# GpSimd's final store waits in reversed order, in a layer norm without affine part

## Chip, cores, metric

The kernel runs on one core of a Trainium2 chip. The metric is the device time of one execution in microseconds, median of several. A profile's span goes from the core's first to its last recorded instruction; the time of a run of this kernel is some 1.8 to 1.9 us longer than its span. A wait is called **met** when its semaphore has reached the value waited for before the engine comes to it.

## The reference

```python
def setup_inputs():                 # x: 32 x 512 x 1024 float32, 67 MB
    ...
def reference(x, eps):
    mean = np.mean(x, axis=-1, keepdims=True)
    var = np.var(x, axis=-1, keepdims=True)
    return ((x - mean) / np.sqrt(var + eps)).astype(np.float32)
```

## The kernel before

The 16384 rows are cut into 17 tiles: fifteen of 8 rows per partition, one of 6, one of 2. A ring of 48 rows per partition holds six large tiles. SP issues the loads (ScalarE half of the first), VectorE takes the statistics, GpSimd combines them, ScalarE normalizes in place and issues the stores. Each store adds 16 to a semaphore `stored[t]`, and SP refills a place of the ring when its store has landed. Everything is inside one critical section. At its end GpSimd waits for those stores that nobody else waits for: tiles 10 to 16, the last owners of the ring.

```python
TILES = (8,) * 15 + (6, 2)
SLOT, SLOTS = 8, 6
...
    ctx.enter_context(tc.tile_critical(no_gpsimd_drain=True))
...
    # ScalarE, for every tile t
                nc.scalar.dma_start(
                    out=rows_of(o2, row, K)[:, a - at : a - at + n, :], in_=ring[:, a : a + n, :]
                )._wait_ge(act, row + k - at + 1).then_inc(stored[t], 16)
...
    for t in range(len(plan)):
        if t in owner.values():                       # tiles 10 to 16
            nc.gpsimd.wait_ge(stored[t], sixteens(stored, t))
# the critical section, then the kernel, ends here
```

## Time and profile before

| | before |
|---|---|
| time, median of 3 runs | 317.93 us (317.60 to 318.04) |
| span of the profiled run | 316.04 us |
| last increment of the last store's semaphore | 314.96 us |
| from there to the end of the span | 1.087 us |

The fourth row is what this document is about, and it is called the **tail**. It is read from the trace: the time of the sixteenth increment of `stored[16]`, taken from the end of the last recorded instruction. The profile's lines for this stretch are in the prediction.

### The profile page before, as it was taken

To read this page: it belongs to the slowest core of one execution; us is meant where nothing else is said; L and a number is where in the kernel's file an instruction comes from. 1 tells how busy PE (TensorE), PEld (TensorE's weight loads), DVE (VectorE), ACT (ScalarE), POOL (GpSimd) and SP (SyncE) were. 2 spreads that over 40 slices of the span, in tenths; PEclk is the share of its full clock that TensorE was granted. 3 is DMA by queue.
4 is the path that set the end of the run, shared out by engine and by line. 5 is a ranking of instruction groups with operands and counts; after the bars stand their busy time and mean duration, and the time that the engine had idled before them with its cause. 6 is when DMAs were issued, how large, how long until landed. Compare 5 with 4: busy or idle time off the path is not lost.

```text
span 316.0 us, 713 instructions
## 1 busy us (share of the span) xinstructions
DVE 156.4 (49%) x273; ACT 153.0 (48%) x146; POOL 41.7 (13%) x176
## 2 busy tenths in 40 slices
DVE  0296595956191651907529084380934709283000
ACT  1006695865834709256091651907429083383800
POOL 0002202022002020020200202011020110204300
DMA  7999999999999999999999999999999999999996
GB/s 294 435 460 402 452 406 402 461 398 465 399 466 402 460 415 448 431 431 452 411 456 406 456 406 456 406 460 402 464 402 460 406 441 452 429 434 425 448 399 285
DMA packets 5043, 134.24 MB, mean 425 GB/s; under 512 B 560, under 2 KB 560, under 8 KB 560
## 3 DMA queue, kind: packets, MB, share of 16 engines
q10 hardware_dynamic: 2592, 69.21, 50.9%
q1 hardware_dynamic: 2448, 65.01, 47.9%
q14 instruction: 3, 0.02, 0.0%
HBM read 67.11 MB, written 67.11 MB: 425 GB/s over the span
## 4 chain that ended last, share of the span: by engine, by line
DMA 61%; DVE 18%; ACT 9%; POOL 5%; issue 2%; ACTq 0%; DVEq 0%; POOLq 0%; SPq 0%
DMA ring<-in_x_dram 32%; DMA out_dram<-ring 29%; DVE stats L119 17%; ACT ring L215 9%; POOL rstd L187 1%; POOL dev L177 1%; POOL dev L181 1%; ACT std L205 0%; POOL dev L173 0%; POOL nmean L170 0%; POOL dev L174 0%; POOL half L166 0%; POOL half L182 0%; POOL nmean L167 0%; POOL ss L183 0%
## 5 line engine op out<-in xcount | busy, mean ns | idle before, releaser
L119 DVE BATCH_NORM_STATS2 stats<-ring 128x6 f32<-128x512 f32 x256 | 153.5, 677 | 86.1 <-DMA ring<-in_x_dram 85.5
L215 ACT ACTIVATE ring<-ring,nmr,rstd 128x1024 f32<-128x1024 f32 x128 | 146.6, 1226 | 11.2 <-POOL nmr L190 11.2
L205 ACT ACTIVATE std<-ss,eps_t 128x8 f32<-128x8 f32 (+2 forms) x17 | 5.1, 300 | 135.1 <-POOL ss L183 134.7
L166 POOL TENSOR_TENSOR half<-stats 128x16 f32<-128x16 f32 (+2 forms) x17 | 4.0, 233 | 232.3 <-DVE stats L119 232.3
L130 DVE RECIPROCAL rstd<-std 128x8 f32<-128x8 f32 x15 | 3.0, 203 | 48.5 <-ACT std L205 48.5
L177 POOL TENSOR_SCALAR dev<-dev 128x32 f32<-128x32 f32 (+2 forms) x17 | 5.0, 295 | 1.5
L190 POOL TENSOR_TENSOR nmr<-nmean,rstd 128x8 f32<-128x8 f32 (+2 forms) x17 | 3.5, 205 | 9.9 <-DVE rstd L130 9.7
L181 POOL TENSOR_TENSOR dev<-dev,stats 128x32 f32<-128x32 f32 (+2 forms) x17 | 4.3, 255 | 1.4
L173 POOL TENSOR_TENSOR dev<-stats,nmean 128x32 f32<-128x32 f32 (+2 forms) x17 | 4.1, 241 | 1.4
L174 POOL TENSOR_TENSOR dev<-dev 128x32 f32<-128x32 f32 (+2 forms) x17 | 4.0, 237 | 1.3
L170 POOL TENSOR_SCALAR nmean<-nmean 128x8 f32<-128x8 f32 (+2 forms) x17 | 4.0, 235 | 1.5
L182 POOL TENSOR_TENSOR half<-dev 128x16 f32<-128x16 f32 (+2 forms) x17 | 3.7, 215 | 1.3
L167 POOL TENSOR_TENSOR nmean<-half 128x8 f32<-128x8 f32 (+2 forms) x17 | 3.4, 202 | 1.3
L183 POOL TENSOR_TENSOR ss<-half 128x8 f32<-128x8 f32 (+2 forms) x17 | 3.4, 202 | 1.3
L187 POOL TENSOR_TENSOR rstd<-std,power 128x6 f32<-128x6 f32 (+1 forms) x2 | 2.1, 1042 | 3.0 <-ACT std L205 3.0
L205 ACT ACT_TABLE_LOAD x1 | 1.3, 1283 | 1.3 <-SPq L55 1.3
L134 DVE MEMSET eps_t<- 128x1 f32 x1 | 0.1, 59 | 1.0 <-SPq L55 1.0
L251 POOL MEMSET const-float32-0.0<- 128x1 f32 x1 | 0.1, 99 | 0.2 <-issue 0.2
L251 POOL MEMSET const-bfloat16-1.0<- 128x1 bf16 x1 | 0.1, 102 | 0.0
L251 POOL MEMSET const-uint8-127<- 128x1 uint8 x1 | 0.1, 102 | 0.0
L251 POOL MEMSET const-float32-1.0<- 128x1 f32 x1 | 0.1, 99 | 0.0
L135 DVE MEMSET power<- 128x8 f32 x1 | 0.1, 65 | 0.0
## 6 DMA issues: line engine op xcount, KB each, us to landing
out_dram<-ring ACTq DMA_DIRECT2D x15, 4096.0 KB, 46.4
ring<-in_x_dram SPq DMA_DIRECT2D x14, 4096.0 KB, 45.5
ring<-in_x_dram SPq DMA_DIRECT2D x1, 3072.0 KB, 43.1
out_dram<-ring ACTq DMA_DIRECT2D x1, 3072.0 KB, 16.0
ring<-in_x_dram ACTq DMA_DIRECT2D x1, 2048.0 KB, 12.6
ring<-in_x_dram SPq DMA_DIRECT2D x1, 2048.0 KB, 12.8
ring<-in_x_dram SPq DMA_DIRECT2D x1, 1024.0 KB, 54.8
out_dram<-ring ACTq DMA_DIRECT2D x1, 1024.0 KB, 14.3
```

The lines of the kernel that those rows point to most:

```text
L119: i = nc.vector.bn_stats(out=stats[:, at + k, s, :], in_=ring[:, at + k, s * BN_MAX : (s + 1) * BN_MAX],)
L166: then(0, g.tensor_tensor(out=h, in0=mean4[:, :, 0:2], in1=mean4[:, :, 2:4], op=ALU.add))
L170: g.tensor_scalar(out=nm, in0=nm, scalar1=-1.0 / H, scalar2=None, op0=ALU.mult),
L173: then(3, g.tensor_tensor(out=d, in0=mean4, in1=spread, op=ALU.add))
L174: then(4, g.tensor_mul(out=d, in0=d, in1=d))
L177: g.tensor_scalar(out=d, in0=d, scalar1=float(D // H), scalar2=None, op0=ALU.mult),
L181: then(6, g.tensor_tensor(out=d, in0=d, in1=m2, op=ALU.add))
L182: then(7, g.tensor_tensor(out=h, in0=d[:, :, 0:2], in1=d[:, :, 2:4], op=ALU.add))
L187: i = g.tensor_tensor(out=r, in0=std_t, in1=power[:, :K], op=ALU.pow)
L190: then(10, g.tensor_mul(out=nmr[:, at : at + K], in0=nm, in1=r), own)
L205: nc.scalar.activation(out=std[:, at : at + K], in_=ss[:, at : at + K], func=AF.Sqrt, bias=eps_t[:], scale=1.0 / D,)._wait_ge(*summed[t]). ...
L215: i = nc.scalar.activation(out=ring[:, k, :], in_=ring[:, k, :], func=AF.Identity, bias=nmr[:, k : k + 1], scale=rstd[:, k : k + 1],).then ...
```

## The change

The intent: after the last store has landed, as little as possible should still have to run. The compiler has made the seven waits into three instructions with two waits each (EVENT_SEMAPHORE in the profile, called wait instructions here) and puts the seventh wait on the branch that leaves the critical section. The first wait in the source's order gets the branch. In the old order that is tile 10, whose store landed 61 us earlier; in the new one it is tile 16, the last.

```diff
-    for t in range(len(plan)):
+    for t in reversed(range(len(plan))):
         if t in owner.values():
             nc.gpsimd.wait_ge(stored[t], sixteens(stored, t))
```

## The prediction

> **What bounds the kernel now.** I read the busy table first, then the DMA rows, then the DMA issues, the last microseconds of the timeline, and last the lines of the waiting instructions. The busy table and the DMA rows of the page say what sets nearly all of the time:
>
> ```profile
> DVE 156.4 (49%) x273; ACT 153.0 (48%) x146; POOL 41.7 (13%) x176
> ...
> DMA  7999999999999999999999999999999999999996
> ...
> HBM read 67.11 MB, written 67.11 MB: 425 GB/s over the span
> ```
>
> No engine is busy for half of the span, while the DMA engines are at 90% or more in every slice but the first and the last. The kernel moves 134 MB at 425 GB/s; that is 316 us. The change touches no transfer, so only the piece after the last byte can move. Where that piece begins is seen in the DMA issues and in the timeline of the last 16 us:
>
> ```profile
> out_dram<-ring ACTq DMA_DIRECT2D x1, 3072.0 KB, 16.0
> out_dram<-ring ACTq DMA_DIRECT2D x1, 1024.0 KB, 14.3
> ```
>
> ```profile
> 299.44 1.22 ACT L215 ACTIVATE ring<-ring,nmr,rstd 128x1024 f32<-128x1024 f32 x1
> 300.69 0.34 ACTq L227 DMA_DIRECT2D out_dram<-ring  x1
> ```
>
> The last store is issued at 300.69 and lands 14.3 us later, at 314.96; the one before it, issued at 296.49, landed at 312.53. The span ends at 316.04. So 1.09 us follow the last landing, and all that the change can touch lies in there. The views by source line show what stands there. First the line of the waits, then those of the end of the critical section and of the kernel's end (columns: line, queue, operation, count, shortest/median/longest duration in ns, first and last start in us):
>
> ```profile
> L234 POOLq EVENT_SEMAPHORE  x3: 42/43/43, 305.3 to 315.0; - x3
> ```
>
> ```profile
> L55 SPq EVENT_SEMAPHORE  x3: 17/17/9061, 235.3 to 292.2; - x3
> ...
> L55 POOLq COMPARE_BRANCH  x1: 38/38/38, 315.1 to 315.1; - x1
> L55 POOLq NOP  x1: 17/17/17, 315.2 to 315.2; - x1
> ```
>
> ```profile
> L265 POOLq EVENT_SEMAPHORE  x4: 17/17/17, 315.4 to 315.9; - x4
> ...
> L265 POOLq COMPARE_BRANCH  x1: 33/33/33, 0.7 to 0.7; - x1
> ```
>
> The reader is to see that GpSimd's seven waits (tiles 10 to 16, which last own a place of the ring) have become three wait instructions, not seven, and that a branch and a NOP of GpSimd follow them. The semaphores of these records, with times to the nanosecond, read:
>
> ```
> 312.553  0.043  event semaphore  waits stored[15], stored[12]
> 314.957         last of the 16 increments of stored[16]
> 314.980  0.043  event semaphore  waits stored[16], stored[11]
> 315.067  0.038  compare-branch   waits stored[10]
> 315.238  0.017  NOP, tells SP
> 315.281  0.013  SP's NOP, which waited for it
> 315.993  0.051  last record of the kernel's end (to 316.044)
> ```
>
> So three instructions carry two waits each, and the seventh wait rides on the branch that leaves the critical section. Written as a list in the source's order, 10 to 16, the branch takes the first and the three pairs are (14,13), (15,12), (16,11). The last store is thus waited for by the third wait instruction, and the branch runs after it although its own store landed at 253.78.
>
> [...] SP's pair on line 55 is recorded as 9061 ns long, most of it the wait for ScalarE. [...] Here GpSimd's branch is recorded as 38 ns and its successor starts 171 ns after it[...].
>
> **The change part by part.** It removes nothing and adds nothing: seven waits, on the same semaphores and values, in the opposite order. If the packing goes by place in the list, the branch takes the first of the new list, stored[16], and the pairs become (12,13), (11,14), (10,15). The number of instructions stays at three waits and a branch.
>
> What moves: the three pairs are done before the end. GpSimd's last arithmetic ends at 298.26; the pair (12,13) is done at once, (11,14) waits until 305.25, (10,15) until 312.53. Allowing 0.1 us for instructions, GpSimd stands at the branch by 312.65, 2.3 us before the last store lands. The branch then starts when a wait instruction would have, at 314.957 + 0.023 = 314.980, instead of 315.067. Removed from behind the last landing are one event semaphore, 0.043 us, and the gap from its end to the branch's start, 315.067 - 315.023 = 0.044 us: together 0.087 us.
>
> Does that reach the end? Everything after hangs on GpSimd: SP's NOP starts at 315.281, 26 ns after the end of GpSimd's NOP, SP's drain and then the closing barrier follow it, and no other engine arrives later on its own account (ScalarE and VectorE had entered the barrier by 301.3 and 292.2). So all of the 0.087 us should come off: 0.03% of 317.93. The sum is 317.93 - 0.09 = 317.84, called 317.85.
>
> **The rivals.** First, a branch that really waits could cost more than one that finds its wait met[...]. Then some of the 0.087 comes back[...]. Against it speaks the kernel's start, where GpSimd's branch on line 265 did wait, for SP: it started 25 ns after the end of SP's NOP, took 33 ns, and the next instruction began 153 ns after its start, not more than the 171 ns of the end. Read the other way, this would save up to 0.02 more: 317.82. The successors differ, so I count neither.
>
> Second, the compiler could order the waits by semaphore or pack them otherwise, so that the machine code is unchanged or the last store sits in a pair again. Then the time is 317.93. The pairs of before are mirrored by list place, which speaks for a rule by place, but since the list is also in order of semaphore number, this trace alone cannot exclude a sort. The title's statement that the branch now has the last store speaks against it.
>
> Third, a second wait within a pair might wake its engine late[...]. After the change stored[14] and stored[15] are such second waits. But there are 2.43 us between the landings of stored[15] and stored[16], so even a microsecond of it stays hidden: 317.84 still. Only stores landing in the other order would spoil this, and the last increments of the two stand 2.4 us apart.
>
> Fourth, the runs' own scatter hides the whole effect: three runs of before lie between 317.60 and 318.04, five times the expected gain. This I hold to be near certain for single runs.
>
> **Range and chances.** The mechanism gives 317.82 to 318.03 over all rivals. The median of a few runs adds some 0.2 us either way, and the median of before that I start from is itself of three runs only, so the range is 317.4 to 318.3. A change of 2% would be 6.4 us, six times all that lies behind the last landing, so faster by that much cannot come from here, and slower only if the transfers changed. Chances: 0.005 faster, 0.99 within 2%, 0.005 slower.
>
> **What would show it.** In the profile after, the line of the waits should still show three event semaphores, but two of them some 7 us long (from 298.4 to 305.3 and from 305.3 to 312.6, because their second waits are the late ones), with the last start at about 305.3 instead of 315.0. The branch on line 55 should start some 0.02 us after the last landing, and from the last landing to the span's end should take 1.00 us instead of 1.09. If that stretch is still 1.09 with the branch first, a waiting branch costs what was saved; if the last event semaphore still starts at the last landing, the packing is another. A time outside the range with that stretch as predicted would be a matter of the transfers and not of this change.

Passages that no trace of this case bears out are cut from the recorded texts (this one and those of `u_first` and `u_second`), and the cuts are marked. The forecast's sum loses no term by it: 317.93 - 0.043 - 0.044 = 317.84 us, called 317.85. Cut from the first rival is its worst case, 0.1 us beyond the 0.087, a guess that was not worked out from a trace. It made the upper end of the 317.82 to 318.03 us that the text gives for all rivals; without it that end is 317.93. The range of 317.4 to 318.3 stands.

## The result

| | before | after |
|---|---|---|
| time, median (6 runs each) | 317.75 us (317.60 to 318.04) | 317.69 us (317.58 to 318.38) |
| span of the profiled run | 316.044 us | 315.747 us |
| last increment of `stored[16]` | 314.957 us | 314.746 us |
| tail | 1.087 us | 1.001 us |

The ratio after to before is 1.000, with a 95% interval of 0.9987 to 1.0013. The forecast of 317.85 us, within 317.4 to 318.3, held; a kernel without any gain would have met it too.

The page of the kernel after shows the same DMA load:

```profile
DMA  7999999999999999999999999999999999999996
...
HBM read 67.11 MB, written 67.11 MB: 425 GB/s over the span
```

The lines of the wait instructions and of the end of the critical section, after (columns as in the prediction: line, queue, operation, count, shortest/median/longest duration in ns, first and last start in us):

```profile
L234 POOLq EVENT_SEMAPHORE  x3: 43/7250/7921, 297.0 to 305.1; - x3
```

```profile
L55 POOLq COMPARE_BRANCH  x1: 38/38/38, 314.8 to 314.8; - x1
L55 POOLq NOP  x1: 17/17/17, 314.9 to 314.9; - x1
```

Against 42/43/43 before, two of the three wait instructions now last 7.9 and 7.3 us, and the last of them starts at 305.1 instead of 315.0: the waiting is done in them, before the last landing. The semaphores and times in the trace, in us from the span's start, duration behind:

```
after                                              before
305.103  7.250  waits stored[10], stored[15]       312.553  0.043  waits stored[15], stored[12]
314.746         last increment of stored[16]       314.957         last increment of stored[16]
                                                   314.980  0.043  waits stored[16], stored[11]
314.771  0.038  branch, waits stored[16]           315.067  0.038  branch, waits stored[10]
314.941  0.017  NOP                                315.238  0.017  NOP
```

In both kernels the first instruction that waits for the last store starts 23 to 25 ns after its last increment. After the change that is the branch itself. From the branch's start to the NOP's start it is 170 ns after and 171 ns before, so the branch that really waits costs no more than the one that finds its wait met.

The two profiled spans differ by 0.297 us. Only 0.086 us of it is in the tail. The other 0.211 us is the last store having landed that much earlier, and the experiments show that this is scatter: among the kernels below, which have the same transfers and arithmetic, the landing lay between 314.69 and 315.23 us, and both ends of that range come from the reversed order (`u_after` and `pad_1`).

### The profile page after: what moved, and what is told of

Read it like the earlier page. It is cut to its first block, busy times and chain, and to the rows that moved or that the text cites. A ratio compares the mean times of both kernels' runs of the same rounds, so it can differ in the third digit from the quotient of the medians. Undisturbed runs are those within 1.5% of the kernel's fastest.

```text
span 315.7 us, 713 instructions
## 1 busy us (share of the span) xinstructions
DVE 156.4 (50%) x273; ACT 153.0 (48%) x146; POOL 41.4 (13%) x176
## 4 chain that ended last, share of the span: by engine, by line
DMA 61%; DVE 18%; ACT 9%; POOL 5%; issue 2%; ACTq 0%; DVEq 0%; POOLq 0%; SPq 0%
DMA ring<-in_x_dram 31%; DMA out_dram<-ring 29%; DVE stats L119 17%; ACT ring L215 9%; POOL rstd L187 1%; POOL dev L177 1%; POOL dev L181 1%; ACT std L205 0%; POOL dev L173 0%; POOL nmean L170 0%; POOL dev L174 0%; POOL half L166 0%; POOL half L182 0%; POOL nmean L167 0%; POOL ss L183 0%
```

## The experiments

**Base.** In all experiments GpSimd's loop over the first twelve tiles is written out, so that its instructions wait on constants and not on a register (a precaution; the arithmetic, the other engines and all transfers are the same). All results were correct against the reference.

```diff
-    count = g.alloc_register("count")
-    ...
-    with g.Fori(0, TURNS):
-        for t in range(SLOTS):
-            combine(t, count)
-            g.reg_add(count, count, 1)
-    for t in range(TURNS * SLOTS, len(plan)):
-        combine(t, t + 1)
+    for t in range(len(plan)):
+        combine(t, t + 1)
```

**Theory.** Only what GpSimd still has to run after the last landing counts. Each wait instruction whose waits are met costs 0.087 us there (0.043 recorded, 0.044 to the next), whereas ahead of the last landing it costs nothing. **Rivals.** The difference of the two tails is chance; met waits behind the one that waits cost nothing; a second wait of a pair wakes late; time in the tail is swallowed by what follows the span.

### Where the last store stands: four orders

The first two runs are the base with the order of before, and with the reversed order.

> The kernel before with GpSimd's loop over the tiles written out (waits on constants), same order of the final waits. It is the base of the other runs. Both theories: machine code of the end is unchanged, so from the last increment of the last store to the end of the span 1.09 us (before: 1.087), one event semaphore of 43 ns starting some 23 ns after that increment, then the branch; the time within 0.3% of before.

> The base with the waits reversed. Theory (each wait instruction behind the last landing costs 0.087 us, and a waiting branch costs no more than one that finds its wait met): stretch from last landing to the end 1.00 us (after: 1.001). Rival (the difference of the two single traces was chance, the stretch varies by a tenth of a microsecond from execution to execution): anything between 0.95 and 1.15.

The next two are base plus one edit each:

```diff
 # u_first
-    for t in range(len(plan)):
-        if t in owner.values():
-            nc.gpsimd.wait_ge(stored[t], sixteens(stored, t))
+    for t in (10, 11, 12, 13, 16, 15, 14):
+        nc.gpsimd.wait_ge(stored[t], sixteens(stored, t))
 # u_second
+    for t in (10, 16, 12, 13, 14, 15, 11):
+        nc.gpsimd.wait_ge(stored[t], sixteens(stored, t))
```

> The base with the order 10, 11, 12, 13, 16, 15, 14, which puts the last store first in the first of the three pairs: two more event semaphores and the branch run after the last landing. Theory: 1.087 + 2 x 0.087 = 1.26 us from the last landing to the end. Rival ([...]met waits cost nothing more and only the first step counts): 1.09 us.

> The base with the order 10, 16, 12, 13, 14, 15, 11: same third pair as before, but the last store is its second wait and not its first. In the profile after, the pair with store 15 second ended 30 ns after the last increment of it (305.103 + 7.250 = 312.353 against 312.323), while a pair with the late store first ended 23 + 43 = 66 ns after it. Theory (only what is left of the instructions after the last landing counts): 1.087 - 0.036 = 1.05 us, event semaphore some seconds of the trace long, about 9.7 us from 305.1 to 314.8. Rival of the prediction[...]: over 1.09 us.

| order | last store is waited for in | tail expected | tail measured |
|---|---|---|---|
| `u_before` | third pair, first wait | 1.09 | 1.076 |
| `u_after` | the branch | 1.00 | 0.990 |
| `u_first` | first pair, first wait | 1.26 | 1.254 |
| `u_second` | third pair, second wait | 1.05 | 1.039 |

The base's tail of 1.076 us is 0.011 us shorter than that of before; 0.009 us of it stands between the branch and the NOP (162 against 171 ns), and why was not looked into. So the base kernels are compared with one another.

The lines of the wait instructions, in `u_before` and in `u_after`:

```profile
L228 POOLq EVENT_SEMAPHORE  x3: 43/43/43, 305.3 to 315.1; - x3
```

```profile
L228 POOLq EVENT_SEMAPHORE  x3: 43/7184/7207, 297.8 to 305.1; - x3
```

The same in `u_first` and in `u_second`:

```profile
L227 POOLq EVENT_SEMAPHORE  x3: 43/43/43, 314.8 to 315.0; - x3
```

```profile
L227 POOLq EVENT_SEMAPHORE  x3: 42/43/2343, 305.2 to 312.6; - x3
```

In `u_first` all three run behind the last landing, from 314.8 on, and each costs as much as expected: 1.254 - 1.076 = 0.178 us for two. So met waits do not run ahead. The reversal saves 1.076 - 0.990 = 0.086 us, as it did in the original pair, so it is not chance. In `u_second` the second wait did not wake late. The instruction's record ends 29 ns after the last increment (312.564 + 2.343 = 314.907 against 314.878), where a pair with the late store first ends 24 + 43 = 67 ns after it; the tail is 0.037 us shorter. One part of that expectation was wrong: I gave the third pair a length of 9.7 us from 305.1, but the pair ahead of it holds GpSimd until store 15 has landed at 312.5, so it lasted 2.34 us.

In time they read 318.34, 317.90, 318.29 and 318.14 us beside 317.88 for before. What stood out is the difference between time and span, 2.2 us in all four against 1.84 and 1.83 us in the profiled runs of before and after. It is taken up below.

### The change made nineteen times as large

A gain of 0.09 us can't be seen in run times that scatter by some tenths. So the wait list was filled to 40 with waits on semaphores met long before. The two kernels have the same instructions in the same number; only the place of the last store differs. Between the two places lie nineteen steps from one instruction to the next, where the change itself has one (the recorded text counts the eighteen met instructions). Each kernel has one of the two `waits` lines shown; the lines that they replace are left out.

```diff
+    done = landed[:3 + SLOTS] + rooted[:3 + SLOTS] + stored[:3] + [later, taken, inverse] + steps[:9]
+    last = (stored[16], 16)
+    keep = [(stored[t], sixteens(stored, t)) for t in range(10, 16)]
+    fill = keep + [(s, 1) for s in done[:34]]
+    waits = fill[:21] + [last] + fill[21:]      # amp_first: second of 20 wait instructions
+    waits = [last] + fill                       # amp_branch: the branch
+    for s, n in waits:
+        nc.gpsimd.wait_ge(s, n)
```

> The change made eighteen times as large. 40 waits in 20 instructions and the branch, nearly all on semaphores that were met long before; the last store is waited for in the second of the 20 instructions, so that 18 met ones and the branch run behind its landing. Theory: 1.076 + 18 x 0.087 = 2.64 us from the last landing to the end, and the time about 1.6 us (0.5%) over that of the same waits with the last store in the branch. Rival (time behind the last landing is absorbed by the runtime's own end, or met waits run ahead): times within 0.3 us of each other.

> The same 40 waits in 20 instructions and the branch, with the last store in the branch. Theory: all 20 instructions are done before the last landing, the stretch is 0.99 us as with seven waits, and the time is that of the reversed base, ratio 0.9997 to before. Rival (each wait instruction costs time wherever it stands): 13 more instructions, some 1.5 us more than the reversed base.

> The base with the waits reversed, once more, now timed against the kernel before. Theory: 0.087 us of 317.8 less, a ratio of 0.9997, so 'same', with an interval that contains 1; stretch from last landing to the end 0.99 us as in its first run. Rival (writing out GpSimd's loop costs time by itself): a ratio above 1.001.

All were timed in five rounds on the same chip, beside nine runs of before (median 317.86 us):

| | median us | ratio to before (95%) | tail us | time less span of the profiled run, us |
|---|---|---|---|---|
| `amp_first` | 319.65 | 1.0052 (1.0038 to 1.0066) | 2.949 | 1.84 |
| `amp_branch` | 317.68 | 0.9990 (0.9976 to 1.0004) | 0.994 | 1.83 |
| `u_after_timed` | 318.05 | 1.0005 (0.9991 to 1.0018) | 0.989 | 2.23 |

The wait instructions and the branch, in `amp_first` and then in `amp_branch`:

```profile
L232 POOLq EVENT_SEMAPHORE  x20: 17/43/43, 297.4 to 316.8; - x20
```

```profile
L55 POOLq COMPARE_BRANCH  x1: 33/33/33, 316.8 to 316.8; - x1
```

```profile
L232 POOLq EVENT_SEMAPHORE  x20: 17/43/13031, 298.0 to 312.9; - x20
```

```profile
L55 POOLq COMPARE_BRANCH  x1: 33/33/33, 315.0 to 315.0; - x1
```

With the last store in the second instruction the wait instructions run on until 316.8, long after the landing at 314.86; with it in the branch the last of them starts at 312.9, before the landing at 314.94, and the branch starts at 315.0. The tails differ by 2.949 - 0.994 = 1.955 us, and the medians by 319.65 - 317.68 = 1.97 us. So time in the tail reaches the measured time in full, and 17 more instructions ahead of the last landing add nothing to the tail (the expectation said 13 more; there are 17). The rival that it is swallowed falls.

The size was a miss, though: expected were 2.64 and a difference of 1.6 us. The starts of the wait instructions in `amp_first` show where the other 0.31 us is. Seventeen of the eighteen steps between wait instructions behind the landing are 86 to 87 ns, but one, between the thirteenth and the fourteenth instruction, is 395 ns (315.841 to 316.236). The same step of 395 ns stands between the same two instructions of `amp_branch` (299.011 to 299.406), where it is hidden behind the waiting.

And two more things did not fit: `u_after_timed` was slower than `amp_branch` by 318.05 - 317.68 = 0.37 us with the same tail, all of it outside the span.

### Where the 0.31 us belongs

From that step on, GpSimd has 17 recorded instructions to the end of the span, and the kernel has 17 more of them than the base. So the step could be tied to a fixed count of GpSimd's instructions, which in the base is reached just behind the span. To test that, one and eleven met wait instructions were added to the reversed base, in three rounds (the diff is shortened; `done` is the list of above):

```diff
     for t in reversed(range(10, 17)):
         nc.gpsimd.wait_ge(stored[t], sixteens(stored, t))
+    for s in done[:2]:          # pad_1; done[:22] in pad_11
+        nc.gpsimd.wait_ge(s, 1)
```

> The reversed base with two waits more, on loads that landed long ago: one instruction more ahead of the branch. It tests why the written-out kernels take some 2.24 us outside the span where before, after and the 40-wait kernels take 1.8 to 1.9, and why both 40-wait kernels show one step of 395 ns instead of 87 between two wait instructions, 17 of GpSimd's instructions before the end, having 17 more than the base. Theory (GpSimd pays some 0.31 us once, at a fixed count of its instructions, which in the base is the first one after the span): the extra step moves into the span, right before GpSimd's last instruction: that step is 0.39 us instead of 0.08, the stretch from the last landing to the end 1.30 us, the time outside the span 1.85 to 1.9 us, and the whole time unchanged at 318.0. Rival (the 0.3 us outside has to do with the runtime's end and not with the count): stretch 0.99, outside 2.24.

> The reversed base with 22 waits more, 11 instructions. Theory: the step of 395 ns now falls right before the last wait instruction, which stands near 305 us, long before the last landing, so it is hidden: stretch 0.99 us, outside the span 1.85 us, and the time 317.7, that is 0.3 us under the reversed base with seven waits although 11 instructions are added. Rival (more instructions cost more, or the 0.3 us stays outside): 318.0 or more.

| | median us | tail us | time less span of the profiled run, us |
|---|---|---|---|
| `pad_1` (one instruction more) | 318.07 | 1.300 | 1.84 |
| `pad_11` (eleven more) | 317.71 | 0.994 | 1.83 |

The instructions of the kernel's end, reversed base (line 259) and `pad_1` (line 261), the same code two lines apart:

```profile
L259 POOLq EVENT_SEMAPHORE  x4: 17/17/17, 315.1 to 315.6; - x4
```

```profile
L261 POOLq EVENT_SEMAPHORE  x4: 17/17/17, 315.6 to 316.4; - x4
```

The four are 0.5 us apart from first to last in the base and 0.8 us in `pad_1`. In `pad_1` the last step is 0.389 us (316.031 to 316.420), in the reversed base 0.078 us (315.505 to 315.583 in the timed run), so the extra 0.31 us has come into the span at the place forecast, and the time outside fell to that of before, 1.84 us. The trace also shows the step where the base should have it: semaphore events go on behind the span, and in `u_after_timed` two increments of semaphore 2 there are 0.650 us apart (315.956 to 316.606), as in the other base kernels with seven waits. The same two are 0.21 us apart in before, after, `amp_branch` and `pad_11`, and 0.26 in `pad_1`. One difference stays open: the time outside fell by 2.23 - 1.84 = 0.39 us, the tail rose by only 0.31.

In `pad_11` the step stands ahead of the last wait instruction, which starts at 305.477, 0.353 us after the end of the one before it, where 0.044 is usual. There it delays nothing, for the last store lands at 314.828:

```profile
L230 POOLq EVENT_SEMAPHORE  x14: 43/43/6956, 297.8 to 305.5; - x14
```

The tail is 0.994, and the kernel with eleven more instructions measured 317.71 us. That is 0.34 us under the 318.05 us of the reversed base in the other series, on another occasion and another chip, and 0.36 us under `pad_1` of the same rounds (all runs of `pad_11` lie between 317.65 and 317.78, all of `pad_1` between 317.87 and 318.36). Against before in these rounds (median 318.03) neither is clear of the noise: ratios 0.9988 (0.9966 to 1.0010) for `pad_11` and 0.9996 (0.9974 to 1.0019) for `pad_1`. So in these written-out kernels GpSimd pays about 0.31 us once, at a fixed count of its instructions, and whether it shows depends on whether the engine is waiting for something else then. What it is was not measured. In the traces of `amp_first`, `amp_branch`, `pad_1` and `pad_11` a packet of 8192 bytes on the DMA queue that the page calls "instruction" is read after it, 0.7 to 3.6 us later; whether the two belong together was not tested.

### The last store waited for behind the barriers

The tail's largest part is not the waits but what stands between the branch and the end (0.98 of 1.00 us in the kernel after, 314.771 to 315.747): the NOP handshake with SP and the kernel's closing barrier in two rounds. So the next version waits for store 16 behind all that, as GpSimd's very last instruction.

```diff
-    for t in range(len(plan)):
-        if t in owner.values():
-            nc.gpsimd.wait_ge(stored[t], sixteens(stored, t))
+    for t in range(10, 16):
+        nc.gpsimd.wait_ge(stored[t], sixteens(stored, t))
+    return [(stored[t], sixteens(stored, t)) for t in (16,)]
 ...
     with _tile.TileContext(nc) as tc:
-        tile_layer_norm_no_affine_kernel(tc, *args)
+        waits = tile_layer_norm_no_affine_kernel(tc, *args)
+    for s, n in waits:
+        nc.gpsimd.wait_ge(s, n)
```

A first form, which ended the critical section by hand and put the wait between its end and the end of the context, did not build: a deadlock was reported.

> A version that may beat both: GpSimd waits for stores 10 to 15 as before inside the section, and for the last store in a wait after the closing barriers of the kernel, so that the way out of the critical section and the barriers run while the last store is still on its way. Theory: the stretch from the last landing to the end is 0.023 + 0.017 = 0.04 us, some 0.95 us less than with the waits reversed, and the time falls by as much: 316.8, a ratio of 0.997 to before. Rival (the time of a run ends with something behind the instructions that is not moved by them): the span falls and the time does not, ratio 1.000.

The lines of the end of the critical section, of the barriers and of the late wait:

```profile
L55 POOLq COMPARE_BRANCH  x1: 32/32/32, 312.3 to 312.3; - x1
```

```profile
L259 POOLq EVENT_SEMAPHORE  x4: 17/17/17, 312.7 to 313.2; - x4
```

```profile
L262 POOLq EVENT_SEMAPHORE  x1: 17/17/17, 314.8 to 314.8; - x1
```

The branch goes as soon as store 15 has landed, at 312.3, the barriers are done by 313.2, and one instruction of 17 ns follows the last landing at 314.768. The tail is 0.041 us, as expected. The time is 316.82 us (316.66 to 316.91), ratio 0.9964 with 0.9950 to 0.9977: 1.04 us less than the 317.86 of before, where the tails differ by 1.087 - 0.041 = 1.046. Its five runs all lie under the fastest of the nine of before, 317.59. This is below the 2% that counts as faster, but clear of the scatter, and it beats both kernels. Its time outside the span is 1.85 us, so the 0.31 us does not show there: by the count it falls at the late wait, where GpSimd waits for 1.6 us anyway. That last point was not tested by itself, but the trace fits it: the two increments of semaphore 2 are 1.80 us apart here (313.544 to 315.345), so the second stands behind GpSimd's wait, and from the start of GpSimd's last instruction to it pass 0.55 us, where `u_after_timed` has 1.02. One thing to check before copying this: the closing barrier holds an instruction that the profile calls EVENT_SEMAPHORE_RANGE_CLEAR (69 ns, from 312.9). In this trace the semaphores that change right with it are 147 to 151 (312.926 to 312.948), and `stored[16]` is 131. A late wait on one of those that change there was not run.

## Why the prediction was right

**The bound.** Transfers set 315 of 316 us, and the change can move only the tail: held, with the same 425 GB/s in both.

**The packing.** Three pairs (12,13), (11,14), (10,15) and the branch with 16: held, to be read from the semaphores of the trace. The rival of a sort by semaphore number falls.

**The size.** Forecast were 0.087 us and a tail of 1.00 us; measured 1.001 us, 0.086 us less. The base pair gave 0.086 us as well, and two more wait instructions behind the landing 0.178 us.

**A waiting branch is dearer.** Falls: 170 ns from its start to the next instruction against 171 ns.

**A second wait wakes late.** Falls, and the sign was the other way: 0.037 us sooner in `u_second`. The forecast did not need it.

**Scatter hides the gain in time.** Held: the interval of the ratio, 0.9987 to 1.0013, is some five times wider either way than 0.086 of 317.8 us, 0.0003. The run time of the change itself therefore shows nothing; the tails and the enlarged pair do.

**One detail was off.** I had two wait instructions of 7 us start at 298.4 and 305.3, behind GpSimd's last arithmetic. They started at 297.1 and 305.1, and the first lasted 7.9 us. Most of the 1.3 us at the first is that GpSimd's last product itself ended 0.98 us sooner in this execution (297.278 against 298.257). The rest is an error of mine: I had every wait instruction start behind the arithmetic ahead of it in the program. In the kernel after, the first starts at 297.047, before the last product, which starts at 297.082, and in `pad_1` one starts at 298.293, the last product at 298.330. Nothing in the sum depended on it.

## What to carry to other kernels

At the end of a kernel, write down what still has to run after the last transfer has landed, and have the last transfer waited for by the very last of these instructions: the order of the waits was worth 0.09 us here, and moving the last wait behind the barriers 1.05 us. An effect smaller than the scatter is measured on the trace from the event that starts it, and its way into the time is shown by making it many times larger. When two kernels with the same end differ by a fixed third of a microsecond, look outside the span and at the instruction count before explaining it by the edit.
